# Masks, ones rows and maxima fields moved ahead, and new transfer durations in the planner of a mixer kernel

## The chip, the core and the metric

The kernel runs on one core of a Trainium2 chip. The metric is the device time of one execution in microseconds; the kernel before has a median of 1007.99 us over 3 runs (1006.95 to 1009.85). The core's engines are named as in the profile: PE is TensorE's matmul (a transpose is a matmul against the identity), PEld its weight load, DVE is VectorE, ACT is ScalarE, POOL is GpSimd, SP is SyncE, which here only issues transfers.

## The reference, cut to what matters

One layer on x of 1024 tokens by 1024 channels, with 16 learned meta tokens put ahead (1040 rows in all):

```python
h = rms_norm(h_res, pre_norm_g)
z = h @ w_in                       # one projection, 7328 columns
(pv, pg, cq, ckv, kr, mg, cu, cg, sbcx, sg, gl) = split_cols(z)
y_a = (pool_mixer(pv, pool_w, pool_scale) * silu(pg)) @ w_out_pool
y_b = (mla_attention(cq, ckv, kr, ...)    * silu(mg)) @ w_out_mla
y_c = (conformer_conv(cu, ...)            * silu(cg)) @ w_out_conf
y_d = (short_conv(sbcx, sc_dw_w)          * silu(sg)) @ w_out_sc
gts = sigmoid(gl + gate_bias)             # four gates of 1024 channels
m = gts[0] * y_a + gts[1] * y_b + gts[2] * y_c + gts[3] * y_d
out = h_res + rms_norm(m @ w_o, post_norm_g)   # meta tokens dropped
```

The attention has 8 heads. Query and key of a head have 64 channels of their own and 32 rotary ones; the rotary key (32 rows) is shared by all heads. Scores are causal, the softmax runs over the keys, V has 64 channels. All is float32.

## The kernel before, in words

**Precision.** Most matmuls split both operands in a high part (type fp32r) and the rest, and add three products: high by high, high by low, low by high. So most matmuls come in threes, and each split costs a copy and a subtraction on other engines.

**The planner.** The program does not issue its instructions as it is written. A class `Plan` records each operation with its engine, a modelled duration (`Plan.cost`, L272) and what it depends on, and `Plan.flush` (L334) runs through modelled time: whenever an engine is free, it takes the ready operation of the lowest priority number. That number is the place in the record, made earlier by `with plan.ahead(n)`. A transfer is modelled in two parts: a `bytes` duration (L279), during which it holds one modelled pipe that all transfers share, and a landing time behind it (L414); `plan.slow(ns)` shifts that landing for the transfers of a block. At most 8 transfers of SP and ACT may be under way in the model. All instructions are issued by one line, L332, so nearly every row of the profile says L332, and one goes by tile names. `plan.hold` keeps a tile's memory from being given away.

Where the model finds PE idle ahead of the first projection unit, it puts in a filler, a transpose of a constant into the bank `ps_w` (`keep_busy`, L260). The number of fillers is fixed when the program is built; on the chip they run whether or not there is a gap.

There are two plans that matter here, one for the start and the projection, one for attention.

**Start.** The 1024 tokens come as 8 tiles x of 128 rows, worked in four pairs (t, t+4). For each pair (`parts`, L755) ACT squares, POOL takes the power that gives 1/rms (tile `rsx`), DVE scales, PE transposes into the operands T and B in the banks `ps_x` and `ps_y`. The first two weight blocks (`raw`, for the columns ckv and kr) are split by POOL into the tiles `kv` and `kr`. Then `sums_of` (L766) makes differences of the x tiles on POOL (rows `x<-x`). The first unit of matmuls needs the first two pairs.

**Projection.** The other 28 blocks of 256 columns are done by a Strassen-Winograd scheme, seven products in place of eight for each, in the banks `ps_pa` to `ps_pd`. Between the products side work is pumped in four lanes: the convolutions, the pooling, Q, K and V of all heads (`task_q`, `task_kv`, `task_so`) and splits of the output weights (`task_w`). Their results go to DRAM; `kr_dram` is the shared rotary key.

**Attention.** Each of 8 heads has two chunks c of 512 queries: 16 units. K lies in two buffers `kt` (even and odd heads), of 100 rows: 64 of the head, 32 rotary and 4 rows of ones. Q lies in `qt` with the same rows; the last four hold the negated row maxima, one row for each 128 queries, so that the score matmul subtracts the maximum itself. `maxima` (L1302) fills them ahead of each unit: scores of all queries at single precision (PE), the mask added (DVE), maxima by blocks of keys into the field `mx` (DVE, 128 x 4 x 3, set to a large negative number first by POOL), then `mr`, the maximum over blocks. One PE transpose turns `mr` [128,4] into [4,128], and a DVE product with `negd`, a mask of -1 on a block diagonal, spreads it over the four rows of `qt`. `attend` (L1335) then makes the scores transposed, adds the mask on the diagonal block (DVE), the exponential (ACT), the split (POOL) and the products with V in `ps_o`. Between these steps, `fills` (L1413) puts the output products of the three other branches: 288 matmuls `ps_y<-bo,whl`, each six of them followed by gating on DVE against the tile `th`. The last head takes the reciprocal of its sums by PE transposes (`ps_y<-ident,ol`, `ps_y<-ident,lcp`).

Before the first unit the program loads Q, the first head's K rows, the rotary rows of the first buffer, and V; in the loop it loads the second head's K, its rotary rows (the two halves of 16 exchanged) and V.

**Output.** The products of the attention branch (`ps_u`), the merge, w_o by the same seven-product scheme, the second norm and the residual.

## Time and profile before

| | us |
|---|---|
| median of 3 runs (range) | 1007.99 (1006.95 to 1009.85) |
| the profiled execution | 1008.78 |
| its span, first to last instruction | 1007.1 |
| PE busy in the span | 983.7 |
| POOL busy | 688.1 |
| DVE busy | 685.0 |
| ACT busy | 448.3 |
| mean granted clock of PE | 0.994 |
| first projection product begins | 53.97 |
| first product of the attention output begins | 874.30 |

The profile is one execution. Its first part gives the busy time of each engine, with the number of instructions behind an x. The table by stage has one row for each stretch of time: start and end, the length, the busy time of the five engines in the order PE, PEld, DVE, ACT, POOL, the mean granted clock of PE (1.00 is full speed), the busy share of the transfer engines, and GB/s. A row of the waits has the waiting group, what released it, the sum of these waits in us, their number and the longest. A row of the timeline has the start, the time from the start of the first to the end of the last of the group, the engine, the operation with its tiles (out<-in), its shape and how many stand in a row; in brackets, how long the engine stood before it, and for whom. Stages: 0 to 55 us is the start, up to 650 the projection, up to 690 the way into attention, up to 875 attention, the rest the output.

### The profile page before, as it was taken

What the parts mean: (1) busy time and instruction counts of PE and PEld (TensorE: products, weight loads), DVE (VectorE), ACT (ScalarE), POOL (GpSimd) and SP (SyncE); (2) the same over time, 40 slices, a digit from 0 to 9 for tenths busy, and PEclk for the clock granted to TensorE, in tenths of its full rate; (3) what the DMA queues carried; (4) which work ended last, traced back from release to release, by engine and by line L of the source; (5) the groups of instructions that cost most, each with busy time, mean ns of one, the idle gap of its engine ahead of it and who ended that gap; (6) DMA issues with size and microseconds to landing.
All of it is one profiled execution on the core that took longest, in us unless ns stands there. A gap on an engine that the chain in (4) does not pass through costs nothing.

```text
span 1007.1 us, 15176 instructions
## 1 busy us (share of the span) xinstructions
PE 983.7 (98%) x5091; PEld 826.2 (82%) x5091; DVE 685.0 (68%) x1106; ACT 448.3 (45%) x895; POOL 688.1 (68%) x640
## 2 busy tenths in 40 slices
PE   9999999999999999999999999989999999999996
PEld 8999898889888878887877888868887878688885
DVE  5855695997899499444455453266677698598747
ACT  7633234443444545444444444215664655424632
POOL 6767876766777668667777676124588785846956
PEclk9999999999999999999999999999999999999998
DMA  7268756678775865766655556895757771572634
GB/s 248 76 219 281 247 169 190 194 244 294 242 248 186 283 215 177 241 176 191 204 178 187 175 167 167 293 267 161 235 175 224 212 232 54 209 242 72 207 118 167
DMA packets 126302, 203.13 MB, mean 202 GB/s; under 512 B 19650, under 2 KB 79161, under 8 KB 124880
## 3 DMA queue, kind: packets, MB, share of 16 engines
q1 hardware_dynamic: 121600, 185.38, 58.6%
q10 hardware_dynamic: 4336, 15.73, 4.2%
q8 instruction: 40, 0.66, 0.3%
q0 software_dynamic: 288, 1.05, 0.3%
q14 instruction: 38, 0.31, 0.1%
HBM read 128.40 MB, written 73.72 MB: 201 GB/s over the span
## 4 chain that ended last, share of the span: by engine, by line
PE 90%; DVE 4%; issue 2%; POOL 2%; DMA 1%; ACT 0%; SPq 0%; DVEq 0%; POOLq 0%; ACTq 0%
PE ps_pa L332 16%; PE ps_pb L332 16%; PE ps_pc L332 15%; PE ps_o L332 9%; PE ps_pd L332 8%; PE ps_u L332 7%; PE ps_s L332 7%; PE ps_y L332 6%; PE ps_x L332 4%; PE ps_w L332 1%; DMA kt<-kr 1%; POOL pt L332 1%; DVE mx L332 1%; DVE a L332 1%; DVE op L332 0%
## 5 line engine op out<-in xcount | busy, mean ns | idle before, releaser
L332 PE MATMUL ps_pb<-T,S 128*128 128x512 f32 (+2 forms) x792 | 172.4, 362 | 0.8 <-DVE u L332 0.8
L332 PE MATMUL ps_pa<-B,A 128*128 128x512 f32 (+2 forms) x792 | 172.2, 362 | 0.0
L332 POOL TENSOR_TENSOR S<-ss,S 128x512 fp32r<-128x512 f32 x84 | 110.5, 1328 | 77.2 <-ACT S L332 77.0
L332 PEld LDWEIGHTS ps_pa<-B,A 128*128 128x128 f32 x792 | 134.6, 188 | 24.4 <-issue 0.5
L332 PEld LDWEIGHTS ps_pb<-T,S 128*128 128x128 f32 x792 | 133.8, 188 | 24.4 <-DVE u L332 1.2
L332 POOL TENSOR_TENSOR A<-raw,A 128x512 fp32r<-128x512 f32 x84 | 117.0, 1398 | 48.2 <-ACT A L332 42.2
L332 POOL TENSOR_TENSOR pt<-p,pt 128x512 fp32r<-128x512 f32 (+4 forms) x112 | 106.1, 976 | 41.6 <-ACT pt L332 27.8
L332 ACT ACTIVATE S<-ss 128x512 fp32r<-128x512 f32 x84 | 50.8, 628 | 115.7 <-DVE ss L332 73.0
L332 PE MATMUL ps_y<-bo,whl 128*128 128x512 f32 x288 | 87.9, 410 | 1.3 <-DVE th L332 1.3
L332 DVE SCALAR_TENSOR_TENSOR ps_w<-conv,par,ps_w 128x512 f32<-128x512 f32 x116 | 87.2, 752 | 2.4
L332 PE MATMUL ps_pc<-B,S 128*128 128x512 f32 (+2 forms) x396 | 87.5, 364 | 0.5 <-DVE z L332 0.5
L332 PE MATMUL ps_pc<-T,S 128*128 128x512 f32 (+2 forms) x396 | 86.4, 363 | 0.4 <-DVE z L332 0.4
L332 ACT ACTIVATE p<-ps_s 128x512 f32<-128x512 f32 (+4 forms) x112 | 49.9, 446 | 82.1 <-DVE ps_s L332 30.9
L332 PE MATMUL ps_pd<-T,A 128*128 128x512 f32 (+2 forms) x396 | 84.9, 361 | 0.0
L332 PEld LDWEIGHTS ps_pc<-T,S 128*128 128x128 f32 x396 | 67.1, 188 | 13.2 <-issue 1.0
L332 PEld LDWEIGHTS ps_pc<-B,S 128*128 128x128 f32 x396 | 66.9, 188 | 13.2 <-issue 1.0
L332 PE MATMUL ps_o<-pt,vt 128*128 128x512 f32 (+4 forms) x336 | 76.2, 332 | 0.8 <-POOL pt L332 0.6
L332 PEld LDWEIGHTS ps_pd<-T,A 128*128 128x128 f32 x396 | 66.9, 188 | 11.9
L332 PE MATMUL ps_s<-qt,kt 100*128 100x512 f32 (+4 forms) x336 | 71.9, 333 | 2.1 <-DVE qt L332 2.1
L332 ACT ACTIVATE A<-raw 128x512 fp32r<-128x512 f32 x84 | 52.7, 627 | 37.0 <-PE ps_pd L332 23.0
L332 PEld LDWEIGHTS ps_s<-qt,kt 100*128 100x128 f32 x336 | 56.6, 184 | 14.7 <-DVE qt L332 3.4
L332 PEld LDWEIGHTS ps_o<-pt,vt 128*128 128x128 f32 x336 | 52.7, 174 | 13.3 <-POOL pt L332 2.3
(344 smaller groups left out, 1895.1 us busy)
## 6 DMA issues: line engine op xcount, KB each, us to landing
raw<-in_w_in_dram SPq DMA_DIRECT2D x56, 512.0 KB
th<-th SPq DMA_DIRECT2D x32, 512.0 KB
th<-z ACTq DMA_DIRECT2D x30, 512.0 KB
v<-vhl SPq DMA_DIRECT2D x16, 384.0 KB
qt<-q SPq DMA_DIRECT2D x16, 384.0 KB
vt<-v SPq DMA_DIRECT2D x8, 768.0 KB
bo<-bo SPq DMA_DIRECT2D x6, 1024.0 KB
kt<-k SPq DMA_DIRECT2D x8, 520.0 KB
```

The lines of the kernel that those rows point to most:

```text
L332: getattr(self.handle[o["eng"]], o["op"])(*map(real, o["args"]), **{k: real(v) for k, v in o["kw"].items()})
```

## The change

What it does:

- **Transfer durations** in the planner: a transfer's `bytes` time has a floor of 0.0432 ns for a byte (before the division by 16); its landing is 3000 ns behind the pipe, where it was 4500 ns and `bytes` once more; the block that loads the x tiles has its landing 400 ns earlier, where it was 2000.
- **Maxima fields**: four tiles `mx`, one for each chunk and parity of the head, are set once at the start of the program; before, each of the 16 units set its own.
- **Negated maxima as diagonals**: `negd` becomes a small diagonal, [128,4,4], made at the start. `mr` times `negd` gives `md` [128,4,4] on DVE; four PE transposes, one for each block of 128 queries, give all [4,512] values in one bank, and a copy on ACT brings them into `qt`.
- **Masks**: `maskS` and `maskT` are made by POOL in the first plan, in a pool of tiles `wr` that lives through both plans, where they were the first POOL work of the second. The tiles `g8`, `pw` and `wraw`, two buffers, move into the same pool.
- **Ones rows**: the 4 rows of ones (and of zeros for the low part) become rows of `kr_dram`, of which there are two now, the second with its halves exchanged. `task_kv` writes them with 8 transfers (before 2) and sets the rows in its tiles with two POOL memsets. The two POOL memsets on `kt` go.
- **Rotary rows first**: each K buffer gets its 36 rows in one transfer, the first behind the first head's loads, the second behind the second load of Q, both ahead of the loop. In the order of issue the planner may exchange them with others.

```diff
@@ -276,7 +276,7 @@
             run = 4 * min(v.shape[-1], w.shape[-1])
-            return {"SP": 450, "ACT": 350, "POOL": 1000}[eng], n * (0.0235 + 35 / run) / 16
+            return {"SP": 450, "ACT": 350, "POOL": 1000}[eng], n * max(0.0432, 0.0235 + 35 / run) / 16
         n = max(size(v) for v in outs + [v for v in ins if isinstance(v, View)])
@@ -411,7 +411,7 @@
                     o["done"] = self.pipe = max(self.pipe, t) + o["bytes"]
-                    land = self.pipe + o["bytes"] + 4500 + min(0, o["extra"])
+                    land = self.pipe + 3000 + min(0, o["extra"])
                     o["end"] = land + max(0, o["extra"])
@@ -480,6 +480,13 @@
     par = const.tile([P, NPAR + 2], F32, name="par")
+    mxs = [[const.tile([P, 4, 3], F32, name=f"mx{c}{e}") for e in range(2)] for c in range(2)]
+    for t in mxs[0] + mxs[1]:
+        POOL.memset(t, NEG)
+    negd = const.tile([P, 4, 4], F32, name="negd")
+    POOL.memset(negd, -1.0)
+    POOL.affine_select(out=negd, in_=negd, compare_op=ALU.is_equal, fill=0.0,
+                       base=0, pattern=[[1, 4], [-1, 4]], channel_multiplier=0)
     z_dram = {}
@@ -493,7 +500,7 @@
     k_dram = [dram.tile([P, 2, L], F32R, name=f"k{g}") for g in range(4)]
-    kr_dram = dram.tile([32, 2, L], F32R, name="kr")
+    kr_dram = [dram.tile([36, 2, L], F32R, name=f"kr{e}") for e in range(2)]
     v_dram = [dram.tile([4, P, 9, 192], F32R, name=f"v{g}") for g in range(2)]
@@ -507,6 +514,8 @@
+    keep = ExitStack()
+    wr = pool(keep, name="wr", reuse_waits="tile")
     one = ExitStack()
@@ -705,9 +714,9 @@
         SP.dma_start(xt[t], a["x"][0, P * t:P * (t + 1), :])
-    g8 = tp.tile([KD, P], F32, tag="wraw", bufs=2, name="g8")
-
-    with plan.slow(-2000):
+    g8 = wr.tile([KD, P], F32, tag="wraw", bufs=2, name="g8")
+
+    with plan.slow(-400):
         load_x(0)
...
@@ -1096,12 +1105,15 @@
         yield
-        kh = t4([32, L], F32R, name="krh")
-        copy(kh, k0)
-        ld(kr_dram[:, 0], kh)
-        kl = t4([32, L], F32R, name="krl")
-        sub(POOL, kl, k0, f(kh))
-        ld(kr_dram[:, 1], kl)
+        kh, kl = t4([36, L], F32R, name="krh"), t4([36, L], F32R, name="krl")
+        for t, v in ((kh, 1.0), (kl, 0.0)):
+            POOL.memset(f(t[32:]), v)
+        copy(kh[:32], k0)
+        sub(POOL, kl[:32], k0, f(kh[:32]))
+        for i, t in enumerate((kh, kl)):
+            ld(kr_dram[0][:, i], t)
+            for r, s, n in ((0, 16, 16), (16, 0, 16), (32, 32, 4)):
+                ld(kr_dram[1][r:r + n, i], t[s:s + n])
         yield
@@ -1235,6 +1247,11 @@
             pass
+    maskS, maskT = (wr.tile([P, P], F32, tag="wraw", bufs=2, name=n) for n in ("maskS", "maskT"))
+    for t, s in ((maskS, 1), (maskT, -1)):
+        POOL.memset(t, 0.0)
+        POOL.affine_select(out=t, in_=t, compare_op=ALU.is_ge, fill=NEG, base=0, pattern=[[-s, P]], channel_multiplier=s)
+    plan.hold([maskS, maskT])
     plan.flush()
@@ -1261,19 +1278,7 @@
     m_ = [[mpair[c][d // 2][:, d % 2] for d in range(KD)] for c in range(2)]
-    maskS = qk.tile([P, P], F32, name="maskS")
-    POOL.memset(maskS, 0.0)
-    POOL.affine_select(out=maskS, in_=maskS, compare_op=ALU.is_ge, fill=NEG,
-                       base=0, pattern=[[-1, P]], channel_multiplier=1)
-    maskT = qk.tile([P, P], F32, name="maskT")
-    POOL.memset(maskT, 0.0)
-    POOL.affine_select(out=maskT, in_=maskT, compare_op=ALU.is_ge, fill=NEG,
-                       base=0, pattern=[[1, P]], channel_multiplier=-1)
-
-    negd = qk.tile([4, 4, P], F32, name="negd")
-    POOL.memset(negd, -1.0)
-    POOL.affine_select(out=negd, in_=negd, compare_op=ALU.is_equal, fill=0.0,
-                       base=0, pattern=[[-1, 4], [0, P]], channel_multiplier=1)
+
     NA = QK + 4
@@ -1284,17 +1289,9 @@
     vt = [qk.tile([P, 9, 192], F32R, name=f"vt{i}") for i in range(2)]
-    for i in range(2):
-        POOL.memset(f(kt[i][QK:NA, 0, :]), 1.0)
-
     def load_kv(h):
         ld(k_[:64].rearrange("p s n -> p (s n)"), k_dram[h // 2][64 * e:64 * (e + 1)].rearrange("p s n -> p (s n)"))
-        if h == 0:
-            ld(k_[64:96], kr_dram)
-        if h == 1:
-            ld(k_[64:80], kr_dram[16:])
-            ld(k_[80:96], kr_dram[:16])
         v = v_dram[h // 4][h % 4]
@@ -1305,8 +1302,7 @@
         q_, k_ = qt[h, c], kt[h % 2]
-        mx = at.tile([P, 4, 3], F32, tag="mx", bufs=2, name="mx")
-        POOL.memset(mx, NEG)
+        mx = mxs[c][h % 2]
         for r in range(4):
@@ -1324,10 +1320,12 @@
         DVE.tensor_reduce(mr, mx, axis=AX.X, op=ALU.max)
+        md = at.tile([P, 4, 4], F32, tag="md", bufs=2, name="md")
+        DVE.tensor_tensor(md, mr.unsqueeze(2).to_broadcast([P, 4, 4]), negd, op=ALU.mult)
         pm = bank("s")
-        PE.transpose(pm[:4, :P], mr, ident)
-        DVE.tensor_tensor(q_[QK:NA, 0, :].rearrange("p (r n) -> p r n", n=P),
-                          pm[:4, :P].unsqueeze(1).to_broadcast([4, 4, P]), negd, op=ALU.mult)
+        for r in range(4):
+            PE.transpose(pm[:4, P * r:P * (r + 1)], md[:, r], ident)
+        copy(q_[QK:NA, 0, :], pm[:4])
         yield
@@ -1472,7 +1470,9 @@
     load_kv(0)
+    ld(kt[0][64:], kr_dram[0])
     load_q(*seq[1])
+    ld(kt[1][64:], kr_dram[1])
     lead_to(0)
@@ -1499,8 +1499,10 @@
     plan.hold(kept)
+    plan.hold([maskS, maskT], -1)
     plan.flush()
     two.close()
+    keep.close()
```

Counted over the program: PE's fillers go from 88 to 109 and the transposes of maxima from 16 to 64; DVE keeps its number (16 products of 128x16 in place of 16 of 4x512); ACT has 16 copies of 4x512 more; POOL has 12 memsets of `mx` fewer; SP issues 8 transfers into `kr_dram` in place of 2, and 2 rotary loads into `kt` in place of 3.

The order moves at three places that the next section speaks of. The first is the start, on POOL, from the first power on. `rsx` is the power for a pair of x tiles, `raw`, `kv` and `kr` belong to the first weight blocks, `x<-x` are the differences. Before:

```order
L332 TENSOR_TENSOR rsx<-rsx,mhalf 128x2
L332 COPY raw<-raw 128x4x16 x2
L332 TENSOR_TENSOR kv<-raw,kv 128x512
L332 COPY raw<-raw 128x4x16 x2
L332 TENSOR_TENSOR rsx<-rsx,mhalf 128x2
L332 TENSOR_TENSOR kv<-raw,kv 128x512
L332 TENSOR_TENSOR kr<-raw,kr 128x256 x2
L332 TENSOR_TENSOR x<-x 128x512 x3
L332 TENSOR_TENSOR rsx<-rsx,mhalf 128x2
L332 TENSOR_TENSOR x<-x 128x512 x4
L332 TENSOR_TENSOR rsx<-rsx,mhalf 128x2
```

And now:

```order
L332 TENSOR_TENSOR rsx<-rsx,mhalf 128x2
L332 COPY raw<-raw 128x4x16 x2
L332 TENSOR_TENSOR x<-x 128x512
L332 COPY raw<-raw 128x4x16 x2
L332 TENSOR_TENSOR kv<-raw,kv 128x512 x2
L332 TENSOR_TENSOR kr<-raw,kr 128x256 x2
L332 TENSOR_TENSOR rsx<-rsx,mhalf 128x2
L332 TENSOR_TENSOR x<-x 128x512
L332 TENSOR_TENSOR rsx<-rsx,mhalf 128x2
L332 TENSOR_TENSOR x<-x 128x512 x8
L332 TENSOR_TENSOR rsx<-rsx,mhalf 128x2
```

The second power moved behind one difference, both `kv` and both `kr`; the fourth moved behind eight differences.

On PE at the same place (`ps_w` is a filler, `ps_x` and `ps_y` with x the transposes of the tiles), from the first pair's transposes into `ps_y` on, before:

```order
L332 MATMUL ps_y<-ident,x 128x128 x4
L332 MATMUL ps_w<-ident 128x128 x2
L332 MATMUL ps_x<-ident,x 128x128 x4
L332 MATMUL ps_w<-ident 128x128 x10
L332 MATMUL ps_x<-ident,x 128x128 x4
L332 MATMUL ps_w<-ident 128x128 x10
L332 MATMUL ps_y<-ident,x 128x128 x4
```

And now:

```order
L332 MATMUL ps_y<-ident,x 128x128 x4
L332 MATMUL ps_w<-ident 128x128
L332 MATMUL ps_x<-ident,x 128x128 x4
L332 MATMUL ps_w<-ident 128x128 x6
L332 MATMUL ps_x<-ident,x 128x128 x4
L332 MATMUL ps_w<-ident 128x128 x43
L332 MATMUL ps_y<-ident,x 128x128 x4
```

The fillers, which stood in groups of up to 10 between the first pairs, now stand 43 in a row ahead of the second pair's first transposes into `ps_y`.

The second place is the way into attention on PE, behind the first three score matmuls of the first unit. `ps_s<-kt,qt` are the scores for the maxima, `ps_s<-ident,mr` the transpose of the maxima. Before:

```order
L332 MATMUL ps_y<-bo,whl 128x512 x50
L332 MATMUL ps_s<-kt_6726,qt 128x264
L332 MATMUL ps_y<-bo,whl 128x512
L332 MATMUL ps_s<-kt_6726,qt 128x328
L332 MATMUL ps_y<-bo,whl 128x512 x2
L332 MATMUL ps_s<-kt_6726,qt 128x328
L332 MATMUL ps_y<-bo,whl 128x512
L332 MATMUL ps_s<-kt_6726,qt 128x392
L332 MATMUL ps_y<-bo,whl 128x512 x2
L332 MATMUL ps_s<-kt_6726,qt 128x392
L332 MATMUL ps_s<-ident,mr 4x128
L332 MATMUL ps_s<-kt_6726,qt 128x456
```

And now:

```order
L332 MATMUL ps_y<-bo,whl 128x512 x4
L332 MATMUL ps_s<-kt_6782,qt 128x264
L332 MATMUL ps_y<-bo,whl 128x512 x2
L332 MATMUL ps_s<-kt_6782,qt 128x264
L332 MATMUL ps_y<-bo,whl 128x512 x2
L332 MATMUL ps_s<-kt_6782,qt 128x328
L332 MATMUL ps_y<-bo,whl 128x512 x3
L332 MATMUL ps_s<-kt_6782,qt 128x328
L332 MATMUL ps_y<-bo,whl 128x512
L332 MATMUL ps_s<-kt_6782,qt 128x392 x2
L332 MATMUL ps_s<-ident,md 4x128 x4
L332 MATMUL ps_s<-kt_6782,qt 128x456
```

Fifty y matmuls in a row became two; the transpose of the first unit's maxima stands behind 12 of them in all, where 60 stood ahead of it.

The third place is the end of attention on PE, from the last products with V to the first products of the attention output (`ps_u`). Before:

```order
L332 MATMUL ps_o<-pt,vt_6914 64x144
L332 MATMUL ps_o<-pt,vt_6914 128x16 x2
L332 MATMUL ps_o<-pt,vt_6914 64x16
L332 MATMUL ps_y<-ident,ol 128x64 x4
L332 MATMUL ps_y<-ident,lcp 64x128 x4
L332 MATMUL ps_u<-boM_8050,whl 128x512 x3
```

And now:

```order
L332 MATMUL ps_o<-pt,vt_6861 64x16
L332 MATMUL ps_y<-bo,whl 128x512 x29
L332 MATMUL ps_y<-ident,ol 128x64 x4
L332 MATMUL ps_y<-ident,lcp 64x128 x4
L332 MATMUL ps_y<-bo,whl 128x512 x18
L332 MATMUL ps_y<-ident,ol 128x64 x4
L332 MATMUL ps_y<-ident,lcp 64x128 x4
L332 MATMUL ps_u<-boM_8021,whl 128x512 x3
```

The last 47 y matmuls, which stood between earlier steps of the last head, now stand behind its last product with V and between its two pairs of sums, and the first pair moved there from an earlier place.

More of the change, by code (lines that the diff above doesn't have):

```diff
@@ L969, in task_pool @@
         s_ = slice(512 * c, 512 * (c + 1))
-        pw = tp.tile([P, P], F32, tag="wraw", bufs=2, name="pw")
+        pw = wr.tile([P, P], F32, tag="wraw", bufs=2, name="pw")
         POOL.memset(pw, 0.0)
@@ L1000, in task_w @@
     def task_w(n, i, d):
-        raw = tp.tile([P, 2, P], F32, tag="wraw", bufs=2, name="wraw")
+        raw = wr.tile([P, 2, P], F32, tag="wraw", bufs=2, name="wraw")
         ld(raw, a[n][0, 2 * P * i:2 * P * (i + 1), P * d:P * (d + 1)].rearrange("(k p) c -> p k c", p=P))
```

## The prediction

> **What bounds the kernel now.** I read the page's first part, then the busy time by stage, then the waits of TensorE.
>
> ```profile
> PE 983.7 (98%) x5091; PEld 826.2 (82%) x5091; DVE 685.0 (68%) x1106; ACT 448.3 (45%) x895; POOL 688.1 (68%) x640
> ...
> 0.00:55.00 55.00, 52.51 (x434) 51.03 (x435) 36.87 (x67) 37.84 (x78) 39.96 (x48) 1.00 0.51 163
> 55.00:650.00 595.00, 592.18 (x3010) 499.00 (x3009) 387.43 (x539) 247.60 (x471) 410.75 (x363) 1.00 0.67 215
> 650.00:665.00 15.00, 15.00 (x68) 12.24 (x67) 7.58 (x15) 1.18 (x2) 5.40 (x12) 1.00 0.82 287
> 665.00:690.00 25.00, 21.85 (x94) 17.24 (x93) 14.38 (x40) 10.14 (x22) 8.39 (x11) 0.86 0.60 157
> 690.00:850.00 160.00, 156.94 (x842) 130.28 (x841) 122.46 (x295) 90.97 (x203) 119.27 (x131) 1.00 0.67 199
> 850.00:875.00 25.00, 22.58 (x115) 17.09 (x114) 18.11 (x30) 10.85 (x22) 16.35 (x13) 1.00 0.52 179
> 875.00:1007.00 132.00, 122.61 (x539) 99.29 (x537) 98.13 (x126) 49.69 (x100) 88.01 (x64) 0.98 0.48 164
> ```
>
> Columns are length, then busy time of PE, PEld, DVE, ACT and POOL, the granted clock, the DMA share and GB/s. TensorE (PE) is busy 98% of the span. So every matmul added to its queue is paid in full, and every other engine matters only where it makes PE wait. The idle time of PE is the length less the busy time: 2.5 us in the start, 2.8 in the projection, none up to 665, 3.2 up to 690, 3.1 in the middle of attention, 2.4 at its end, 9.4 in the output stage. Only the stage from 665 to 690 has a low clock: 0.86 over 25 us is 3.5 us of lost work on top of the idle.
>
> ```profile
> PE ps_s L332 <- DMA kt<-kr: 2.2, 1, 2.2
> PE ps_s L332 <- DVE qt L332: 2.1, 4, 1.1
> PE ps_w L332 <- POOL mhalf L332: 1.4, 1, 1.4
> PE ps_y L332 <- DVE th L332: 1.3, 2, 0.8
> ...
> PE ps_s L332 <- DVE mx L332: 0.9, 2, 0.5
> ...
> PE ps_y L332 <- ACT ol L332: 0.7, 1, 0.7
> PE ps_o L332 <- POOL pt L332: 0.6, 2, 0.4
> ...
> PE ps_y L332 <- DVE lcp L332: 0.3, 1, 0.3
> ```
>
> The longest single wait is for the rotary rows of the second K buffer, 2.2 us. What it does to the clock one window shows:
>
> ```profile
> 677.00:678.00 1.00, 1.00 (x5) 1.00 (x6) 0.61 (x2) 0.00 (x0) 0.00 (x0) 0.50 1.06 383
> ```
>
> PE is busy again, at half clock. The waits of 1.1 us and less elsewhere leave their stages at 1.00.
>
> The Trainium skill ("TensorE: Matmul & The Clock Gate", section "Why this matters for your kernels") asks for no idle gap above some 3 us between matmul bursts. By that rule this gap of 2.2 us would have left the clock alone, and removing it would be worth 3.5 us less. The row says otherwise, so the row goes into the sum.
>
> **The change, part by part.**
>
> *Start.* The new transfer durations give every queue another order; the start is where it costs. PE's filler transposes grow from 88 to 109.
>
> ```profile
> 1.44 3.51 PE L332 MATMUL ps_w<-ident 128*128 128x128 f32 x17 [1.44 <-POOL mhalf L332]
> ...
> 6.51 3.66 PE L332 MATMUL ps_w<-ident 128*128 128x128 f32 x32
> 10.00 0.60 PE L332 MATMUL ps_x<-ident,x 128*128 128x128 f32 x4
> ...
> 14.39 0.63 PE L332 MATMUL ps_y<-ident,x 128*128 128x128 f32 x4
> ```
>
> Warm, 32 fillers take 10.00 - 6.51 = 3.49 us, 0.109 each; 21 more are 2.3 us. Why are there more? POOL's power for the second pair of x tiles (the second `rsx`) now stands behind a subtraction on x, both kv splits and both kr splits.
>
> ```profile
> 10.53 0.41 POOL L332 COPY raw<-raw 128x64 f32<-128x64 f32 x2 [2.16 <-DMA raw<-in_w_in_dram]
> ...
> 12.43 0.42 POOL L332 COPY raw<-raw 128x64 f32<-128x64 f32 x2
> 12.80 0.71 POOL L332 TENSOR_TENSOR rsx<-rsx,mhalf 128x2 f32<-128x2 f32 x1
> 13.46 1.30 POOL L332 TENSOR_TENSOR kv<-raw,kv 128x512 fp32r<-128x512 f32 x1
> 14.70 1.45 POOL L332 TENSOR_TENSOR kr<-raw,kr 128x256 fp32r<-128x256 f32 x2
> ...
> 20.78 5.27 POOL L332 TENSOR_TENSOR x<-x 128x512 f32<-128x512 f32 x4
> 26.01 0.69 POOL L332 TENSOR_TENSOR rsx<-rsx,mhalf 128x2 f32<-128x2 f32 x1
> ...
> 13.54 0.75 DVE L332 SCALAR_TENSOR_TENSOR x<-x,rsx,ps_pc 128x512 f32<-128x512 f32 x1
> ```
>
> From the landing at 10.53: copies 0.41, subtraction 1.3, copies 0.4, two kv 2.5, two kr 1.45, power 0.7, which ends at 17.2 (before: 13.5). The scaling on DVE behind it takes 0.75, so PE gets the second pair at 18.0 instead of 14.39. On PE 37 fillers and 16 transposes of x come after 6.51, 53 x 0.109 = 5.8, to 12.3; the run of 43 fillers lasts 4.7 more, to 17.0. That leaves 1.0 us idle. The fourth pair's power now waits behind eight more subtractions (1.32 each by the row at 20.78): it ends near 30.3 (before 26.7), and PE, which comes there near 30.7, waits some 0.5. Slots and smaller steps: 0.5. Gone are the old waits of this stage, 2.5 less the 1.4 for the identity = 1.1. Sum: 2.3 + 1.0 + 0.5 + 0.5 - 1.1 = **+3.2**. From below: fillers alone, old waits gone, +1.2. From above: the whole delay of 3.6 us and the 0.5 and 0.5, +4.6.
>
> *Projection.* The two masks (four POOL instructions under 0.3 us each), the maxima fields, the ones rows (two POOL memsets of about 1 us, now near 125 us) and six more small transfers lie beside a PE that is 99.5% busy. POOL has 410.75 of 595 us to do, so they are hidden; uncovered they would cost 3 us once. All else is reordered. I take **0**: 2.8 us of idle can go or double, -1.5 to +2.8.
>
> *Maxima.* Each of the 16 units had one transpose of the row maxima; it has four now, 48 more. What does one cost?
>
> ```profile
> 850.39 0.94 PE L332 MATMUL ps_y<-bo,whl 128*128 128x512 f32 x3
> 851.17 0.27 PE L332 MATMUL ps_s<-ident,mr 128*4 128x128 f32 x1
> 851.20 1.17 PE L332 MATMUL ps_y<-bo,whl 128*128 128x512 f32 x4
> ...
> 860.13 0.60 PE L332 MATMUL ps_y<-ident,lcp 128*64 128x128 f32 x4
> 860.49 0.48 PE L332 MATMUL ps_y<-bo,whl 128*128 128x512 f32 x1
> ```
>
> The next matmul starts 0.03 us after the single one; four in a row with 64 columns, not 4, take 0.36, 0.09 each. Four in a row are nearer to the second: 0.07, so **+3.4** (1.4 to 4.3). Off PE: the product on DVE (0.68 below) becomes one of 128x16, like the reduction `mr` (0.17), and a copy on ACT (like `ol`, 0.60).
>
> ```profile
> 666.32 0.17 DVE L332 TENSOR_REDUCE mr<-mx 128x4 f32<-128x12 f32 x1
> ...
> 680.54 0.68 DVE L332 TENSOR_TENSOR qt<-ps_s,negd 4x512 fp32r<-4x512 f32 x1 [2.54 <-PE ps_s L332]
> ...
> 678.94 0.60 ACT L332 ACTIVATE ol<-ps_o 128x512 f32<-128x512 f32 x1 [4.74 <-PE ps_o L332]
> ```
>
> DVE loses 16 x 0.5 = 8 us, ACT gains 10 in a stage where it works 91 of 160 us. The copy queues behind exponentials on ACT, and the first score matmul of its unit waits for it; the y matmuls between cover that.
>
> *Into attention.* The rotary rows of both K buffers are issued before the V tile, so the wait of 2.2 us ends, and with it the half clock: **-3.5**. With the masks ready, the first maxima start at once, and only 12 y matmuls, not 60, stand ahead of the first transpose. What is late next is DVE's chain:
>
> ```profile
> 664.14 1.47 DVE L332 TENSOR_REDUCE mx<-ps_s 128x1 f32<-128x144 f32 x4
> 665.52 0.29 DVE L332 TENSOR_TENSOR ps_s<-ps_s,maskS 128x128 f32<-128x128 f32 x1
> ```
>
> Five reductions 1.9 us, four mask additions 4 x 0.33, `mr` and the diagonal 0.4: 3.6 us, then 0.9 for transposes and copy. PE has 12 y and 9 score matmuls against it, some 4 us. I expect 1.3 us of waits, in pieces, where 3.0 stood (2.2, and of the waits for `mx` and `qt` 0.8): **-1.7** (-2.7 to +0.5).
>
> *Middle of attention.* Of 3.1 us idle, 1.8 are waits for `qt` on DVE, which loses work: **-0.8** (-2 to +1.5).
>
> *End of attention.* Before, the y matmuls run out; now 47 of them stand around the last head's transposes. The idle of 2.4 us becomes waits of y for DVE, which needs two instructions of 0.7 for every six y: 0.8 left, **-1.6** (-2.3 to 0).
>
> *Output stage.* Same instructions, a few neighbours exchanged: 0 (-0.5 to +0.5).
>
> **Sum:** 3.2 + 3.4 - 3.5 - 1.7 - 0.8 - 1.6 = **-1.0**. The profiled execution took 1008.78 us (span 1007.1), so 1007.8; it lay 0.8 above the median of the runs, 1007.99. Predicted median: **1007.0**.
>
> **Rivals.** 0.3%, 3 us, is about what a measurement of this kernel can tell from no change: faster means below 1005, slower above 1011.
>
> *A, faster.* Four short transposes pipeline as the single one did (0.03 each): 2.0 less. And the start costs only its fillers: 2.0 less. 1003.0. For it: the row at 851.17. Against it: the late power on POOL, which no other engine makes good.
>
> *B, slower: the clock falls in the start.* The gap behind the 43 fillers is 1.0 us by the sum. Should the POOL chain be 1 us longer, it is as long as the gap at 675, and half clock follows there too: 1.0 + 3.5 gives 1011.5. It decides from some point between the 1.1 us that left the clock at 1.00 and the 2.2 that did not. Against it: POOL's durations are known.
>
> *C, slower: the wait moves.* If K of the second head (the transfer behind the third th tile) lands late, or DVE's chain leaves one gap of 2 us, the transition keeps its idle and its half clock: 1007.0 + 1.7 + 3.5 = 1012.2. For it: transfers there run at a share of 0.82 to 1.06 of the DMA engines. Against it: K's second load is now issued ahead of the first maxima.
>
> *D, slower: fillers count as idle.* Then the run of 43 with the gap behind it is 5.7 us without work, and the half clock comes whatever the gap: 1007.0 + 3.5 = 1010.5, or more with B. Against it: the rows at 1.44 and 6.51, where nothing but transposes ran and one went from 3.51 / 17 = 0.206 us to 0.109, so they wake the clock here. This rival is the rule of the Trainium skill ("TensorE: Matmul & The Clock Gate", "Part 4: PE-mode transpose") that transposes do not count as activity; the trace disagrees.
>
> **How the numbers follow.** Forecast 0.46, A 0.29, B 0.10, C 0.11, D 0.04. The forecast's own range is 1004.5 to 1010. Faster has A's 0.29 and a little of the forecast, 0.31; slower has B, C, half of D: 0.23; same 0.46. Eight in ten: from a little under A, 1002.5, to B, 1011.5; the rest of A's lower bounds and C's upper lie outside.
>
> **What would show it.** Right: in the changed profile 109 fillers, PE's second y transposes near 18.0 and the first unit's matmuls 3 us later than before; no wait for `kt` and a clock of 1.00 from 650 to 690; the four `md` transposes 0.28 us together; no idle between 865 and 880. The prediction falls if the projection (same matmuls) takes 3 us more or less than 595, which no row here prices, or if a stage shows a clock of 0.5 that had 1.00.

## The result, and the profile after

The change makes the kernel slower: 1016.92 us (median of 8 runs, 1013.48 to 1018.24) beside 1008.77 for the kernel before on the same chip, a ratio of 1.0078 with a 95% interval of 1.006 to 1.0096. The forecast was 1007.0 and its range ended at 1011.5. The profiled execution took 1017.59 us with a span of 1015.9, 8.8 more than the span of before, so it stands for the runs.

The two kernels can be laid beside each other by what PE begins: the first projection product, the first score matmul, the first product of the attention output (`ps_u`). The busy time by stage of the kernel before, cut there (columns as in the prediction: length, PE, PEld, DVE, ACT, POOL, clock, DMA share, GB/s):

```profile
0.00:53.97 53.97, 51.48 (x426) 50.00 (x426) 36.67 (x66) 36.80 (x76) 38.93 (x47) 1.00 0.50 160
53.97:651.59 597.62, 594.80 (x3025) 501.32 (x3024) 387.63 (x539) 249.09 (x473) 412.55 (x365) 1.00 0.67 216
651.59:874.30 222.71, 214.08 (x1105) 174.94 (x1104) 162.22 (x375) 112.68 (x247) 148.64 (x165) 0.98 0.65 196
874.30:1007.10 132.80, 123.31 (x543) 99.91 (x540) 98.44 (x126) 49.69 (x100) 88.01 (x64) 0.98 0.48 165
```

The same view of the changed kernel, and then its parts of attention:

```profile
0.00:57.92 57.92, 54.91 (x446) 53.18 (x447) 38.45 (x66) 37.66 (x77) 39.54 (x54) 1.00 0.49 155
57.92:654.55 596.63, 594.28 (x3025) 500.88 (x3024) 387.98 (x539) 249.88 (x472) 421.52 (x370) 1.00 0.68 217
654.55:883.53 228.98, 218.73 (x1153) 178.79 (x1152) 157.06 (x376) 120.88 (x264) 140.69 (x143) 0.99 0.61 185
883.53:1015.90 132.37, 122.53 (x543) 99.76 (x540) 99.99 (x126) 49.01 (x99) 84.08 (x62) 0.98 0.51 169
...
654.55:665.00 10.45, 9.76 (x50) 7.45 (x49) 9.73 (x28) 3.75 (x7) 1.91 (x3) 1.00 0.92 276
665.00:690.00 25.00, 25.00 (x144) 21.08 (x142) 15.53 (x46) 15.82 (x37) 14.65 (x18) 1.00 0.59 172
690.00:850.00 160.00, 154.31 (x815) 127.34 (x814) 107.49 (x261) 88.60 (x192) 107.05 (x107) 0.98 0.62 186
850.00:883.53 33.53, 29.66 (x149) 22.92 (x149) 24.31 (x45) 12.70 (x28) 17.08 (x17) 1.00 0.48 164
```

The start is 3.95 us longer, the projection 0.99 shorter, attention 6.27 longer, the output 0.43 shorter. In attention the idle time of PE (length less busy) goes from 8.63 to 10.25. Of PE's busy time, the part lost to a low clock (busy time times one less the clock, added over slices of 1 us) is 3.33 before and 3.39 after; busy time less that loss is 210.75 and 215.34. So the 6.27 are 4.59 of work (the 48 transposes), 1.62 of idle and 0.06 of clock. These are net figures. The old wait on the way into attention is gone, with its half clock (no idle and 1.00 from 665 to 690), and the same amounts stand again in the middle: 5.69 idle between 690 and 850, and half clock there. The waits of PE in the changed kernel show for whom:

```profile
PE ps_s L332 <- ACT p L332: 2.8, 1, 2.8
PE ps_s L332 <- DVE mx L332: 2.6, 3, 2.0
PE ps_s L332 <- DVE md L332: 1.7, 1, 1.7
```

The wait for the rotary rows in `kt` is gone, and of the 2.1 us for `qt` 0.7 are left, now for ACT. In their place stand one wait of 2.8 us for the exponential `p` and one of 2.0 for a maximum. What happened at the first, all engines in order of time:

```profile
761.34 1.28 POOL L332 TENSOR_TENSOR pt<-p,pt 128x512 fp32r<-128x512 f32 x1
761.51 3.89 DVE L332 TENSOR_TENSOR op<-ol,rb 64x512 f32<-64x512 f32 x1
762.59 1.04 POOL L332 TENSOR_TENSOR pt<-p,pt 128x400 fp32r<-128x400 f32 x1
763.60 1.25 POOL L332 TENSOR_TENSOR m<-m,th 128x512 f32<-128x512 f32 x1
765.93 0.28 DVE L332 TENSOR_TENSOR ps_s<-ps_s,maskT 128x128 f32<-128x128 f32 x1
766.30 0.40 ACT L332 ACTIVATE p<-ps_s 128x272 f32<-128x272 f32 x1 [4.82 <-DVE ps_s L332]
766.75 0.28 PE L332 MATMUL ps_s<-qt,kt 100*128 100x16 f32 x1 [2.77 <-ACT p L332]
```

The instruction to look at is `op<-ol,rb` on DVE: it divides a head's result `ol` by its softmax sums (`rb` is the reciprocal, spread over 64 rows). Both inputs lie in SBUF. It took 3.89 us, and it ends 0.55 us after the third of three POOL instructions that ran without a break (764.85). Behind it on DVE stood the second product of the pair, which took 0.68, and a mask addition, behind that the exponential on ACT (4.82 idle), behind that PE. The second gap is built in the same way, and its long product too ends 0.55 us after the last of the POOL instructions (819.01):

```profile
815.75 3.81 DVE L332 TENSOR_TENSOR op<-ol,rb 64x512 f32<-64x512 f32 x1
816.00 1.03 POOL L332 TENSOR_TENSOR pt<-p,pt 128x400 fp32r<-128x400 f32 x1
817.00 1.28 POOL L332 TENSOR_TENSOR m<-m,th 128x512 f32<-128x512 f32 x1
818.25 0.76 POOL L332 TENSOR_TENSOR pt<-p,pt 128x272 fp32r<-128x272 f32 x1
821.10 0.43 PE L332 MATMUL ps_s<-kt,qt 96*128 96x348 f32 x1 [1.97 <-DVE mx L332]
```

How long this product takes otherwise shows in the group of the tile `op`; the three times are the shortest, the median and the longest in ns. Kernel before, then changed kernel:

```profile
L332 DVE TENSOR_TENSOR op<-ol,rb x14: 673/685/2178, 732.1 to 876.0; 64x512 f32<-64x512 f32 x14
```

```profile
L332 DVE TENSOR_TENSOR op<-ol,rb x14: 673/685/3892, 722.6 to 872.3; 64x512 f32<-64x512 f32 x14
```

And each of these two gaps is followed by half clock, as a window behind the first one shows for the changed kernel:

```profile
768.00:769.00 1.00, 0.93 (x4) 0.74 (x3) 1.00 (x4) 0.90 (x4) 0.58 (x2) 0.51 0.98 395
```

The dip lasts from 768 to 772, a second one from 822 to 826; each costs some 1.7 us of work.

### The profile page after: what moved, and what is told of

The parts are those of the page before. It is cut to its first block, busy times and chain, and to the rows that moved or that the text cites. A ratio compares the mean times of both kernels' runs of the same rounds, so it can differ in the third digit from the quotient of the medians.

```text
span 1015.9 us, 15352 instructions
## 1 busy us (share of the span) xinstructions
PE 990.5 (97%) x5160; PEld 832.6 (82%) x5160; DVE 683.5 (67%) x1106; ACT 457.4 (45%) x911; POOL 685.8 (68%) x628
## 4 chain that ended last, share of the span: by engine, by line
PE 90%; DVE 5%; issue 2%; POOL 2%; ACT 1%; DMA 0%; DVEq 0%; ACTq 0%; POOLq 0%
PE ps_pb L332 16%; PE ps_pa L332 16%; PE ps_pc L332 15%; PE ps_o L332 9%; PE ps_pd L332 8%; PE ps_s L332 7%; PE ps_u L332 7%; PE ps_y L332 6%; PE ps_x L332 4%; PE ps_w L332 1%; DVE op L332 1%; DVE mx L332 1%; DVE th L332 1%; DVE ps_s L332 1%; DMA raw<-in_w_in_dram 0%
## 5 line engine op out<-in xcount | busy, mean ns | idle before, releaser
L332 POOL TENSOR_TENSOR A<-raw,A 128x512 fp32r<-128x512 f32 x84 | 112.8, 1346 | 76.8 <-ACT A L332 71.4
L332 POOL TENSOR_TENSOR S<-ss,S 128x512 fp32r<-128x512 f32 x84 | 117.3, 1402 | 59.6 <-ACT S L332 57.6
L332 POOL TENSOR_TENSOR pt<-p,pt 128x512 fp32r<-128x512 f32 (+4 forms) x112 | 101.7, 935 | 63.1 <-PE ps_s L332 24.1
L332 PE MATMUL ps_o<-pt,vt 128*128 128x512 f32 (+5 forms) x336 | 75.4, 331 | 0.0
L332 PEld LDWEIGHTS ps_o<-pt,vt 128*128 128x128 f32 (+1 forms) x336 | 53.5, 174 | 11.2 <-issue 0.3
```

What stands on the lines that cost most here:

```text
L332: getattr(self.handle[o["eng"]], o["op"])(*map(real, o["args"]), **{k: real(v) for k, v in o["kw"].items()})
```

## The experiments

Three ideas were on trial. The first: the long `op` products are the loss, and they are long because DVE waits with two SBUF inputs for POOL. Against it: the loss belongs to the new transfer durations alone (called O), or to the diagonals alone (called M). Each comparison is with the kernel before in the same batch. Heads 0 to 6 have such a product for each chunk.

### The product with one input

```diff
         mul(DVE, op[c][64 * e:64 * (e + 1), :], ol[h][:64, c], rb)
+        plan.ops[-1].update(op="tensor_reduce", kw={"axis": AX.X, "op": ALU.max},
+                            args=(op[c][64 * e:64 * (e + 1), :], ol[h][:64, c].unsqueeze(2)))
```

The product is recorded as before, so that the planner gives the same order, and issued as a reduction (a maximum over one element) of `ol` alone. The division by the softmax sums is left out, for heads 0 to 6, where both inputs lie in SBUF, and for the last head too, where the sums lie in PSUM. The order of PE, ACT and POOL is that of the change.

> The changed kernel, in the same order on every engine; only the 14 DVE products op<-ol,rb (two inputs from SBUF) read one input: each is a maximum over one element of ol. Left out: the division by the softmax sum of heads 0 to 6. Theory P (the port): in the changed trace the product at 761.51 took 3.89 us, because three POOL instructions stood back to back from 761.34 to 764.85; the second such product, at 815.75, took 3.81 us. The gaps on PE of 2.8 and 2.0 us and the two half clocks (1.7 us lost each) hang on these. So P expects products near 0.7 us, both gaps and both half clocks gone, 6 to 8.5 us less than the changed kernel: ratio to before 0.999 to 1.002. Rival M (the new maxima path): DVE and ACT are late there because of the diagonals and the copies on ACT; then the gaps stay and the ratio stays near 1.008. Rival T (the transfers, whose share was 0.98 to 1.00 in both gaps): the products stay long with one input too, ratio 1.008.

Measured: 1007.2 us, ratio 0.9983 (0.997 to 0.9997); 9.7 us less than the change. The stage of attention, the place of the first gap, and the group of the tile:

```profile
654.64:874.52 219.88, 215.01 (x1153) 176.36 (x1152) 147.51 (x376) 120.93 (x264) 138.99 (x143) 1.00 0.63 193
```

```profile
761.52 1.26 DVE L332 TENSOR_REDUCE op<-ol 64x512 f32<-64x512 f32 x2
```

```profile
L332 DVE TENSOR_REDUCE op<-ol x16: 666/669/681, 722.6 to 875.4; 64x512 f32<-64x512 f32 x16
```

Attention is 9.1 us shorter than in the change. Idle is 4.87 where it was 10.25, the clock loses nothing where it lost 3.39. No instruction was taken away or moved. The reduction need not wait for `rb`, but it starts at 761.52, where the product started at 761.51; what differs is that DVE reads one input here, and all 16 take 0.67 to 0.68 us. The reduction overwrites the same tile `op` in the same order of POOL, and the transfers run on beside it, so neither a wait for POOL to be done with `op` nor the transfers (rival T) made the products long. So the long products cost the change its two gaps, its two dips and all that it lost to the kernel before. The last head has no part in it: from its `md` transposes to the first `ps_u` it is 28.61 us in the change (854.92 to 883.53) and 28.57 here (845.95 to 874.52).

### The transposes twice

```diff
+        for _ in range(o.get("times", 1)):
...
         for r in range(4):
             PE.transpose(pm[:4, P * r:P * (r + 1)], md[:, r], ident)
+            plan.ops[-1]["times"] = 2
```

> The changed kernel, in the same order; each of the 64 transposes of md is issued twice into the same place. By the changed trace four take 0.35 us until the next matmul starts, 0.0875 each: 64 more cost 5.6 us, ratio to before 1.0135. By the prediction's 0.07 each: 4.5 us, 1.0123. If they hide as the single transpose seemed to (0.03): 1.9 us, 1.0097. Only a wait behind them could make it more.

Measured: 1020.52 us, ratio 1.0113 (1.0096 to 1.013), 3.6 more than the change for 64 more transposes; in single profiles attention is 4.24 longer. What one costs, in the doubled kernel and then in the change (start, length from first start to last end):

```profile
666.15 1.03 PE L333 MATMUL ps_s<-ident,md 128*4 128x128 f32 x8
666.95 0.95 PE L333 MATMUL ps_y<-bo,whl 128*128 128x512 f32 x3
```

```profile
668.86 0.60 PE L332 MATMUL ps_s<-ident,md 128*4 128x128 f32 x4
669.21 0.95 PE L332 MATMUL ps_y<-bo,whl 128*128 128x512 f32 x3
```

Eight take 0.80 us to the next start, four 0.35; so four more cost 0.45, 0.11 each, though each gives 4 rows, not 128. For 48 that is 5.2 us; attention's work rose by 4.59. The whole times of this run would give a smaller price, 3.6 us for 64 transposes, but they hide part of it: attention's work (busy less clock loss) is 6.40 longer here, 0.10 for each of the 64, while one of the two dips did not come (1.70 lost in place of 3.39) and the idle time is 0.47 shorter in attention and 2.2 in the projection.

### The two halves apart

The change with the three old durations, as shown, and the kernel before with the three new ones, the same edit the other way round:

```diff
-            return {...}[eng], n * max(0.0432, 0.0235 + 35 / run) / 16
+            return {...}[eng], n * (0.0235 + 35 / run) / 16
-                    land = self.pipe + 3000 + min(0, o["extra"])
+                    land = self.pipe + o["bytes"] + 4500 + min(0, o["extra"])
-    with plan.slow(-400):
+    with plan.slow(-2000):
```

> The changed kernel with the three old transfer durations in the planner (masks, ones rows, rotary rows and diagonals stay). Theory O (the order of the new durations costs): the start goes back to 54.0 for the first projection product (4 us less), the way into attention stays without its wait and at clock 1.00, the transposes cost 4.6, and the long products in the middle of attention go: about 1007, ratio 0.998. Theory A (the attention's own changes bring the gaps): the start gains 4 and the gaps stay, about 1012.5, ratio 1.004. If the start was repaid later in the projection, 1016, ratio 1.007.

> The kernel before with the three new transfer durations alone. The start loses 4 us and the projection gives 1 back; the wait for the rotary rows and the half clock behind it stay. Theory O: the gaps of 2 to 3 us in the middle of attention come with this order, 1016 or more, ratio 1.007 to 1.010. Theory A: no such gaps, 1008.8 + 3 = 1011.8, ratio 1.003. By the prediction's own start term, +3.2, ratio 1.003.

Measured: with old durations 1005.49 us, 0.9962 (0.9947 to 0.9977); the new durations alone 1023.38, 1.0137 (1.0117 to 1.0156). In the first the longest `op` takes 1.78 us. The group of `op` in the second:

```profile
L332 DVE TENSOR_TENSOR op<-ol,rb x14: 675/1234/5527, 738.9 to 880.9; 64x512 f32<-64x512 f32 x14
```

With old durations the products of 3.8 us are gone and the change gains. The new durations alone have the longest product of all (5.53 us) and moreover a projection 7.7 us longer than before's, 4.1 of it idle. So this looked like theory O.

### The diagonals undone

The old path of the maxima (one transpose, product on DVE into `qt`, the old `negd`) in the change, with old durations and with new:

```diff
...
-        md = at.tile([P, 4, 4], F32, tag="md", bufs=2, name="md")
-        DVE.tensor_tensor(md, mr.unsqueeze(2).to_broadcast([P, 4, 4]), negd, op=ALU.mult)
         pm = bank("s")
-        for r in range(4):
-            PE.transpose(pm[:4, P * r:P * (r + 1)], md[:, r], ident)
-        copy(q_[QK:NA, 0, :], pm[:4])
+        PE.transpose(pm[:4, :P], mr, ident)
+        DVE.tensor_tensor(q_[QK:NA, 0, :].rearrange("p (r n) -> p r n", n=P),
+                          pm[:4, :P].unsqueeze(1).to_broadcast([4, 4, P]), negd, op=ALU.mult)
```

> Masks, maxima fields, ones rows and rotary rows as changed, but one transpose and the DVE product with the old negd for the negated maxima, and the old durations. Against the run with the old durations alone (1005.5 us): 48 transposes fewer. By 0.109 each, the price that eight in a row showed: 5.2 less, about 1000.3, ratio 0.991. If DVE, which gets 16 products of 0.68 back, brings waits of its own, up to 3 of it are given back: 1003.5, ratio 0.994. If the transposes lie beside other work: 1005.5, ratio 0.996.

> The changed kernel with one transpose and the old DVE product for the negated maxima; the new durations stay. If the long products belong to the order of the new durations (theories O and P), some op<-ol,rb still takes over 3 us and PE keeps one or two gaps near 2 us: 5.2 less than the changed kernel for 48 transposes, 1010 to 1013, ratio 1.002 to 1.005. If they came with the diagonals and ACT's copies (rival M), they go: 1002 to 1005, ratio 0.994 to 0.997.

Measured: with old durations 1000.62 us, ratio 0.9923 (0.9896 to 0.9951), faster than both kernels; with new durations 1005.84, 0.997 (0.9956 to 0.9983). The second, its stage of attention and its group of `op`:

```profile
653.38:870.08 216.70, 211.68 (x1105) 172.85 (x1104) 159.32 (x376) 112.36 (x248) 143.77 (x145) 1.00 0.64 195
```

```profile
L332 DVE TENSOR_TENSOR op<-ol,rb x14: 677/972/1805, 715.5 to 859.6; 64x512 f32<-64x512 f32 x14
```

The new durations are there, and no `op` is longer than 1.81 us; theory O falls. Theory M falls by the run with old durations and diagonals. A long wait is not a loss by itself: another product with two SBUF inputs, the sum `m<-m,th`, took 3.11 us in this run and 2.95 at 835.80 in the change, and PE has no gap over 0.3 us in the 5 us behind either:

```profile
824.03 3.11 DVE L332 TENSOR_TENSOR m<-m,th 128x512 f32<-128x512 f32 x1
```

Such a wait costs where PE's next step hangs on DVE soon after, as in the two gaps. Medians, all other edits of the change being in (before: 1008.8):

| | one transpose | four transposes |
|---|---|---|
| old durations | 1000.6 | 1005.5 |
| new durations | 1005.8 | 1016.9 |

From 1000.6, the diagonals cost 4.9, about what the transposes take; the durations cost 5.2, of which 3.3 in the start of the profiled executions. Together they would make 1010.7. The change takes 6.2 more, and of these four only that corner has `op` products of 3.8 us. Neither half makes them here by itself, though on the kernel before the durations alone did: which product meets a run of POOL is a matter of the whole order.

The best of the four has two levels of its own: some executions near 1000.3, others near 1004.5; from the upper level, the part of the change that neither half explains would be 10 and not 6.2. Its profiled one, at 1005.06, lost 5.1 us to half clock behind this (PE in order of time, then a window):

```profile
654.00 0.27 PE L332 MATMUL ps_s<-ident,mr 128*4 128x128 f32 x1 [0.23 <-DVE mx L332]
654.74 0.94 PE L332 MATMUL ps_s<-kt,qt 96*128 96x456 f32 x2 [0.47 <-DVE mx L332]
655.93 4.20 PE L332 MATMUL ps_s<-qt,kt 100*128 100x512 f32 x14 [0.24 <-DVE qt L332]
```

```profile
656.00:657.00 1.00, 1.00 (x3) 0.81 (x4) 0.97 (x3) 0.00 (x0) 0.00 (x0) 0.50 1.05 420
```

Three waits of half a microsecond and less, 0.94 in all, precede a dip of 10 us.

### A break in POOL's run

If DVE waits until POOL pauses, a small POOL instruction that needs the product itself should end the run in time.

```diff
         mul(DVE, op[c][64 * e:64 * (e + 1), :], ol[h][:64, c], rb)
+        POOL.tensor_copy(brk[64 * e:64 * (e + 1)], op[c][64 * e:64 * (e + 1), :1])
```

It was put into the change with old durations, into the version of 1000.6, and into the change:

> The run with the old durations, with one POOL copy of 64x1 behind each DVE product op<-ol,rb that reads its result, so that POOL has to wait there and leaves the port. Theory P: no such product over 1.9 us (1.78 was the longest without), PE's half clock near 764 goes (1.7 us), POOL's 14 waits lie beside PE: 1003.5 to 1005.5, ratio 0.994 to 0.996. Rival: POOL's waits make the splits pt late, and PE waits for pt: 1006 to 1009, ratio 0.997 to 1.000.

> One transpose, the old durations and the POOL copy behind each DVE product. If both earlier expectations hold, 998.5 to 1001, ratio 0.990 to 0.992. If POOL's waits cost, 1002 to 1004. If the gaps come with other DVE instructions of two SBUF inputs (the additions m<-m,th), the break changes nothing against one transpose alone.

> The changed kernel, nothing left out, with one POOL copy of 64x1 behind each DVE product op<-ol,rb that reads its result: POOL has to wait there, and so leaves the port to DVE after at most the instructions that stand ahead of the copy. The order differs in few places, all behind the first such product. Theory P: no product over 2.5 us, the gaps of 2.0 and 2.8 us on PE go with their half clocks, and the time comes near that of the run with one input (1007.2): 1007 to 1010, ratio 0.998 to 1.001. Rival: the long products come from elsewhere, or POOL's waits cost as much: 1014 or more, ratio 1.005.

Measured: 1003.77 (0.9949, 0.9927 to 0.997), 1005.31 (0.9952, 0.9933 to 0.9971) and 1016.77 (1.0082, 1.0064 to 1.0099). In the first it may be worth 1.7 us, but the intervals overlap, the longest `op` is as long as without it (1.78), and the dip near 764 that it was to end stayed (1.7 us of work in both profiles). In the second it costs 4.7 by the medians, more than either forecast, though not in the profiled executions (1002.97 and 1005.06). The change is as slow as without it, against the forecast of 1007 to 1010. What took the place of the gaps in the change with the break:

```profile
766.02 1.17 DVE L332 TENSOR_TENSOR md<-mr,negd 128x16 f32<-128x16 f32 x1
818.58 1.91 DVE L332 TENSOR_TENSOR md<-mr,negd 128x16 f32<-128x16 f32 x1
```

The `op` products are short, none over 1.77 us. The next DVE instruction with two SBUF inputs, the diagonal, then waits: 1.17 and 1.91 us, where the group's median is 0.17, and PE has gaps of 1.14 and 1.35 us behind them. Attention loses 7.77 us to the clock there, more than the change itself.

### The diagonal with one input

```diff
...
-        DVE.tensor_tensor(md, mr.unsqueeze(2).to_broadcast([P, 4, 4]), negd, op=ALU.mult)
+        DVE.tensor_reduce(md.rearrange("p (a b) -> p a b", b=5)[:, :, 0], mr.unsqueeze(2), axis=AX.X, op=ALU.max)
```

`md` is one of two zero tiles here, the reduction writes its diagonal, and the sign goes into the rows of ones of K. Once with the break, once with the one-input `op` (again without the division):

> The run with the break, and the diagonal md made by a DVE reduction that reads one input (mr) and writes the diagonal of a tile of zeros; the rows of ones in K become -1, so nothing is left out. Every engine keeps the order of the run with the break, with a reduction in the place of each of the 16 products md<-mr,negd and two POOL memsets more. Theory P2: with the break the products op<-ol,rb were short (1.77 at most), but md<-mr,negd, 0.17 us alone, took 1.17 and 1.9 us behind POOL's runs just ahead of two of the three gaps; the old product qt<-ps_s,negd, with one input from PSUM, never took more than 0.69. So all gaps near 766, 820 and 851 and their half clocks go: 7.8 of clock and some 3 of idle time less than 1016.8, 1005 to 1009, ratio 0.996 to 1.000. Rival: DVE is late there for its amount of work, whatever the port: the gaps stay, 1013 to 1017, ratio 1.004 to 1.008.

> The changed kernel in its own order, with both kinds of DVE product reading one input: op<-ol (the division by the softmax sum of heads 0 to 6 left out, as in the run with one input) and md<-mr by a reduction. Theory P2: the one gap that the run with one input kept, 1.7 us before the transposes of md near 845, goes too: 1004.5 to 1006.5, ratio 0.995 to 0.998. If md costs nothing in this order, it equals the run with one input, 1007.2, ratio 0.998.

Measured: 1014.34 (1.0054, 1.0034 to 1.0073) and 1007.79 (0.9993, 0.9979 to 1.0007). Both miss what the idea forecast, and fit the rivals. In the first all 16 diagonals take 0.16 us, and the gaps of 1.14 and 1.35 us are gone, but only 2.4 us are gained, with intervals that overlap: a gap of 1.53 us at 851 in the run with the break stands here too (1.55 at 849), PE waits another 1.12 us for `pt` on POOL at 853, and the half clock from 769 on comes without the gap. The second is no better than the run with one input for `op` alone (1007.2): without the breaks the diagonal's second input is worth nothing that these runs can tell. Why the version with both cures stays 6.5 above it is open: clock loss (5.95 in attention) is most of it, and which small wait sets it off was not told apart.

### The power first

```diff
-    rsqrt_mean(rsx[:, 2 * t:2 * t + 2], ssx[:, 2 * t:2 * t + 2], D)
+        with plan.ahead(200 if t else 0):
+            rsqrt_mean(rsx[:, 2 * t:2 * t + 2], ssx[:, 2 * t:2 * t + 2], D)
```

> The changed kernel with one priority added: POOL's power for each later pair of x tiles goes ahead of the kv and kr splits and the differences recorded near it. The planner gives PE 10, 8 and 6 fillers there again in place of 43. If the late second power is what costs the start, the first projection product begins at 54.5 to 55.0 in place of 57.92. If the late thing is something else (the x tiles' arrival, the splits of kv and kr themselves), it stays at 57 to 58. The order behind the start changes too, so the whole time says little: 1009 to 1016 either way, as long products on DVE come or not.

Measured: 1017.49 us, 1.0075 (1.0051 to 1.0099): no gain, though the start did as it was told; the second pair is transposed at 14.21:

```profile
5.94 0.60 PE L332 MATMUL ps_pd<-ident,gC 128*128 128x128 f32 x4
55.12 1.68 PE L332 MATMUL ps_pa<-B,A 128*128 128x256 f32 x12
```

The first product begins 2.8 us earlier than in the change (57.92). Of this 1.2 us are there before the two orders differ on PE: the transposes into `ps_pd`, behind the same instructions, begin at 5.94 here and at 7.15 in the change. The other 1.6 us are the late power's, by this run. The other stages give most of it back: the projection is 1.1 longer, attention 0.9, where three dips cost 5.1 against 3.4.

### A later hand-over in the planner

The version of 1000.6 with a modelled hand-over between engines of 250 ns in place of 150:

```diff
-    WAKE = {"PE": 350, "ACT": 150, "DVE": 150, "POOL": 150, "SP": 0}
+    WAKE = {"PE": 350, "ACT": 250, "DVE": 250, "POOL": 250, "SP": 0}
```

> One transpose, the old durations, and in the planner 250 in place of 150 ns from the end of an instruction of DVE, ACT or POOL to what waits for it. Two more y matmuls stand ahead of the first transpose of maxima, where one transpose alone left three gaps of 0.2 to 0.5 us within 2 us and lost 5.1 us of clock in its profile. If those pieces are covered: 996 to 1000, ratio 0.988 to 0.991. If the other order elsewhere takes it back: 1001 to 1005.

Measured: 1012.84 us, 1.0031 (1.0012 to 1.0049), 12 worse than its base and outside both forecasts; half clock stayed where it was to go, though shorter (from 657 to 661). The order it makes brings waits that no other version has, this one and one of 3.7 us for `kt`:

```profile
PE ps_y L332 <- DMA bo<-bo: 6.7, 1, 6.7
```

This shows how far one number of the planner moves the time by order alone; it cures nothing.

## Why the prediction was wrong

The forecast was -1.0 and the profiled executions differ by +8.8. Step by step, in the prediction's order:

*Start: right in mechanism, 0.75 short* (+3.2, measured +3.95). The rows that answer it, the first of the kernel before, the others of the changed one:

```profile
6.07 0.60 PE L332 MATMUL ps_pd<-ident,gC 128*128 128x128 f32 x4
7.15 0.60 PE L332 MATMUL ps_pd<-ident,gC 128*128 128x128 f32 x4
11.38 1.29 POOL L332 TENSOR_TENSOR x<-x 128x512 f32<-128x512 f32 x1 [1.18 <-PE ps_x L332]
13.38 4.86 PE L332 MATMUL ps_w<-ident 128*128 128x128 f32 x43
16.84 0.72 POOL L332 TENSOR_TENSOR rsx<-rsx,mhalf 128x2 f32<-128x2 f32 x1
18.44 0.63 PE L332 MATMUL ps_y<-ident,x 128*128 128x128 f32 x4 [0.21 <-issue]
```

The power ends at 17.56 (said 17.2), the second pair is transposed at 18.44 (said 18.0). Of the 3.95, 1.08 are chance as far as these runs show: `ps_pd` stands behind the same 27 matmuls of PE in both kernels, but the first fillers were slow for longer in the second profile (a group of 5 took 0.77 us before and 1.33 here), and over all the runs, of either order, this row begins between 5.94 and 7.43. From it to the first product it is 47.90 us before and 50.77 in the change, 2.9 more. That is about the 2.3 of the fillers and 0.5 more idle, so the 0.5 for slots and smaller steps was not there. The gap behind the 43 fillers is 0.21, not 1.0, and 0.20 to 0.48 in the other runs with these fillers, however early PE came to them: the prediction let POOL's chain start at the landing, but its subtraction waits for PE (the row at 11.38). The rivals B and D, half clock behind these fillers, did not come.

*Projection and output: in their bounds* (0 and 0, measured -0.99 and -0.43).

*Maxima: the size of a term was off.* 0.07 was taken for a transpose; they cost 0.10 to 0.11. The work of attention rose by 4.59, not 3.4, beyond the upper bound of 4.3. The prediction had the right row and divided it wrongly: four `lcp` transposes took 0.36 to the next start, and if the first costs 0.03, the other three cost 0.11 each. The bound of 0.09 had spread the cheap first one over all four.

*Into attention: right.* No wait for `kt`, clock 1.00, no idle from 665 to 690 and 0.7 ahead of it: -2.46 of idle and -3.33 of clock, where -1.7 and -3.5 were forecast. The run with one transpose and new durations shows that the gain is real once nothing takes it back: attention lasts 216.70 there, and 222.71 before, with as many matmuls.

*Middle of attention: the step that failed* (-0.8, bounds -2 to +1.5; measured about +6). Idle went from 3.06 to 5.69, and 3.4 us were lost to the clock. The step argued that DVE loses 8 us of work and so would be waited for less. DVE's busy time in attention did fall, from 162.22 to 157.06 us, and PE waited more. The step counted busy time, and did not ask with what DVE's instructions run at the same time. The loss of this stage hangs on two of 14 products, whose median is the same 0.685 us as before; no sum of durations shows them. The row for it stood in the profile of before, where the longest `op` took 2.18 us at a median of 0.685. A spread of three to one in instructions of one shape was the sign to look at what POOL did beside it.

*End of attention: wrong sign* (-1.6, measured +1.45). The new order does stretch the y matmuls over the last head, but PE waits 1.7 us for `md` at 853, in two small pieces for `lcp`, and there are y matmuls that wait for `th`.

The miss of 9.8 us is thus: middle 3.4 of idle and 3.4 of clock, end 3.0, transposes 1.2, start 0.75, less 0.6 on the way in, 1.0 in the projection and 0.4 in the output. None of the rivals had the mechanism. C, a wait that moves, was nearest, but looked for it in the transition and in transfers. The prediction's last sentence, that it falls if a stage shows half clock that had 1.00, is what happened.

## What to carry to other kernels

Before you count what an engine gains, look at the longest instruction of each group, not at its mean: where the longest is three times the median, an order that shifts things by a few us can make it nearly six times, as here. In this kernel the DVE instructions with two SBUF inputs beside a densely busy POOL were such groups; with one input (0.67 to 0.68 us), or one of two in PSUM (0.68), the time stood fixed. And a change to a planner's costs is a change to the whole order: measure it apart from the edits that come with it, for here edits worth 3.3 us and more were hidden under it.

## What the runs showed of the hardware

**DVE can wait through a whole run of POOL.** With two SBUF inputs, `op` took 3.89 and 3.81 us in the change and 5.53 with the new durations alone, beside POOL instructions of 0.8 to 1.3 us each that followed one another at once; all three ended 0.55 us after the last of them. It is not always so. In the change itself, inside a run of POOL:

```profile
723.74 1.77 DVE L332 TENSOR_TENSOR op<-ol,rb 64x512 f32<-64x512 f32 x1
724.94 1.73 POOL L332 TENSOR_TENSOR pt<-p,pt 128x512 fp32r<-128x512 f32 x1
```

This product ended 0.55 us after the first POOL instruction that it met (724.97), and here the next one of POOL was long, 1.73 us where the same shape took 1.28 at 761.34. What decides who goes first was not found. With one input none of 16 took over 0.68. The product into `qt` of the kernel before, with one input in PSUM, was never disturbed either:

```profile
L332 DVE TENSOR_TENSOR qt<-ps_s,negd x16: 682/683/684, 667.7 to 852.2; 4x512 fp32r<-4x512 f32 x16
```

The Trainium skill ("SBUF — State Buffer", section "SBUF: two separate sides") says that such a DVE instruction and a POOL instruction lock a shared pair of ports, and that whichever starts first holds it for its whole instruction. The runs agree on which instructions collide. They add that DVE is not always served at the end of the one that it met: in the first gap it waited for three.

**Half clock does not follow from the length of one gap.** Before, 2.2 us lost 3.3 us of work; in the change 2.77 and 1.97 lost 1.7 each, and 1.74 ahead of the transposes at 854.92 lost nothing. With the power first, nearly the same gap, 1.73 at 852.59, lost 1.7; with the transposes twice, 1.50 at 823.08 lost nothing. Three pieces of 0.94 in all lost 5.1 in the version of 1000.6. Dips last about 3.4, 6.8 or 10 us. The Trainium skill ("TensorE: Matmul & The Clock Gate", section "What's actually happening") has a window of some 3.4 us that runs freely, with no regard to the program; the lengths of the dips fit it, and so would gaps that cost by chance, but no run here shows the window's phase. Such chance may make a few us of difference between executions of one kernel, and so a part of what stays open above; no run here shows two profiles of one kernel.

**A short transpose is not cheap.** It took 0.11 us each in a row, with 4 rows of output, as much as a full one of 128 (the fillers, 0.113 each by the row at 13.38).
